# Another order of the seven score products in a planned decoder-layer kernel, and other durations for its planner

## The chip, the cores and the metric

The kernel runs on one core of a Trainium2 chip. Its engines are TensorE (PE, with its weight loads shown as PEld), VectorE (DVE), ScalarE (ACT), GpSimd (POOL) and the queue that issues the DMAs (SP). The metric is the device time of one execution in microseconds. The kernel before takes 2433.74 us, the median of three runs (2433.09 to 2435.8).

## The reference

One decoder layer over 2048 positions of width 1024, all in float32. A mixer (a gated linear recurrence and a convolution module side by side) is followed by cross-attention into 256 memory positions with four heads, and by a gated feed-forward of width 3072 with a short convolution; a norm ends it. The part that the change touches is the cross-attention:

```python
    h = rms_norm(x, xa_norm_g[l])
    m = rms_norm(mem, mem_norm_g[l])
    q = (h @ w_q[l]).reshape(bsz, s, XA_HEADS, XA_HD)
    kv = m @ w_kv[l]
    ...
    scores = jnp.einsum("bshd,bmhd->bhsm", q, k).astype(jnp.float32) * (XA_HD ** -0.5)
    p = jax.nn.softmax(scores, axis=-1).astype(v.dtype)
    o = jnp.einsum("bhsm,bmhd->bshd", p, v).reshape(bsz, s, d)
    x = x + o @ w_o[l]
```

## The kernel before, in words

**The stages.** The sequence is worked in two halves of 1024 positions. In `attend` (line 1373) each half passes through three large products, one after the other: the mixer's output times `w_out` (the order `FIRST`), the normed activations times a matrix A that holds `w_q` times the keys of all four heads (`SECOND`, the score products), and the probabilities times a matrix VO that holds the values times `w_o` (`THIRD`, the output products). While the first half's attention runs, the second half's recurrence and convolution run on VectorE and ScalarE beside it.

**Seven products for eight.** Each large product is 1024 by 1024 by 1024 and is cut into quarters of 512. `seven` (line 1228) makes it from seven products of 512 by 512 by 512, P1 to P7, whose operands are quarters or sums of quarters: S1 = A21 + A22, S2 = S1 - A11, S3 = A11 - A21, S4 = A12 - S2 on the left, T1 to T4 on the right. The results are gathered into the quarters C11, C12, C21 and C22. Each of the seven runs over four inner blocks `i` (groups) and four blocks of 128 positions `tb`. Every operand is split into a rounded high part and a low rest, so each pair of blocks takes three matmuls of 128 by 128 by 512: 12 matmuls in a group.

**Banks.** A product's four blocks of positions lie in four of the eight banks of PSUM. The orders name them "a" or "b", and say whether the product starts fresh (True) or adds to what the banks hold (False). P1, P6 and P7 add up in "a", and each state of the sum is taken out on the way; P5 and P3 add up in "b". The names after that are the quarters that the product's result goes to. The number `held` counts the banks in use; the recurrences put their gate matmuls only where it is at most 4 (line 990).

**Scores and probabilities.** `score` (line 1432) takes a product's banks: the first result of a quarter is copied to SBUF by ScalarE (tile `prob`), every later one is added by VectorE. With the last one, `softmax` (line 1263) follows for that block of 128 positions: VectorE finds the maximum of two heads, ScalarE takes two exponentials with sums, VectorE the reciprocals, ScalarE scales the two parts. A quarter has four such blocks. `turn` (line 1399) transposes a quarter of probabilities on TensorE, 16 transposes into four banks, and `take_p` (line 1443) copies these out on ScalarE (tile `pt`). The rounding of `pt` gives `yh` on ScalarE, and `yl` on VectorE: the left operands of the output products. The last argument of `seven` says after which product and group such work is put into the program, counted from 0: (6, 0) is after the first group of the seventh product.

**The planner.** The program is not run in the order in which it is written. Every instruction is recorded with its operands (`Program`), and `schedule` (line 320) simulates the five engines with estimated durations (`estimate`, line 66), a hop of 0.3 us between engines, DMA rates, table switches on ScalarE and the free slots of SBUF and PSUM. On each engine the ready instruction with the earliest due time goes first. Due times are worked back from when TensorE wanted the results in the pass before (`deadlines`, line 283). `emit` (line 466) makes 28 passes, takes the pass with the least estimated end, and emits each engine's instructions in that order. All instructions are emitted by one line, so the profile gives line 485 for all of them and is read by the names of tiles.

Of the kernel before, what the change touches and what calls it, by code (L numbers as in the profile page):

```python
# [62 lines left out]
STACKS = 2  # L63


def estimate(eng, name, n, pointer):
    if eng == "DVE":
        if name == "reciprocal":
            return 0.1 + n * 0.0063
        return (0.13 if name == "scalar_tensor_tensor" else 0.08) + n * 0.00104  # L70
    if eng == "Pool":
        return 0.18 + n * 0.0021
    return 0.1 + n * 0.00083 + 0.09 * pointer


class Buf:
# [90 lines left out]
class Program:  # L167
# [51 lines left out]
    def do(self, eng, name, out, *args, reads=(), writes=(), **kw):  # L219
        outs = [out] + ([kw["accum_out"]] if "accum_out" in kw else [])  # L220
        ins = [a for a in list(args) + list(kw.values()) if isinstance(a, Ref) and a not in outs]
        if eng == "PE":
            o = self.group or self.op("PE")
            n = ins[1].n if name == "matmul" else P
            if name == "matmul":
                cost = (n + 32) / 2400.0 if ins[1].rounded else n * 4 / 2400.0
            else:
                cost = 0.11
            self.clock += cost
            o.cost += cost  # L230
        else:
            o = self.op("Pool" if eng == "either" else eng)
            o.either = eng == "either"
            n = max(r.n for r in ins + outs)
            o.cost = estimate(o.eng, name, n, any(isinstance(a, Ref) for a in kw.values()))
            if eng == "DVE":
                self.vector = max(self.vector, self.clock) + o.cost
            if eng == "ACT":
                o.sets = ACT_SETS.get(args[1])
        o.calls.append((name, (out,) + args, kw))  # L240
        for r in outs:
            if not r.rounded:
                r.buf.loaded = False
        self.touch(
            o, [b for r in ins for b in r.parts()] + [b.parts[0] for b in reads],
            [b for r in outs for b in r.parts()] + [b.parts[0] for b in writes],
        )
# [72 lines left out]
    def schedule(self):  # L320
# [9 lines left out]
        def push(t, kind, x):  # L330
            seq[0] += 1
            heapq.heappush(events, (t, seq[0], kind, x))
# [35 lines left out]
        def pick(e, t):  # L368
            h = ready[e]
            while h and h[0][2].start is not None:  # L370
                heapq.heappop(h)
            if not h:
                return None
            if e == "Pool":
                back, o, wake = [], None, None
                while h and o is None:
                    x = heapq.heappop(h)
                    if x[2].start is not None:
                        continue
                    spare = x[2].due + lag[0] - POOL_LAST - t  # L380
                    if x[2].either and spare > 0:
                        back.append(x)
                        wake = spare if wake is None else min(wake, spare)
                    else:
                        o = x[2]
                for x in back:
                    heapq.heappush(h, x)
                if o is None and wake is not None:
                    push(t + max(wake, 0.2), 3, e)
                return o  # L390
            if e == "ACT":
                o = h[0][2]
                if o.sets is not None and table[0] not in o.sets and o.due + lag[0] - t > ACT_PATIENCE:
                    other = [x for x in h if x[2].sets is None or table[0] in x[2].sets]
                    if other:
                        x = min(other)
                        h.remove(x)
                        heapq.heapify(h)
                        return x[2]
            return heapq.heappop(h)[2]  # L400

        def dispatch(e, t):
            if not idle[e]:
                return
            o = pick(e, t)
            if o is None:
                return
            idle[e] = False
            o.start, o.on = t, e
            order.append(o)  # L410
            if e == "PE":
                lag[0] += 0.2 * (t - o.turn - lag[0])
            cost = o.cost
            if e == "ACT" and o.sets is not None and table[0] not in o.sets:
                cost += ACT_SWITCH
                table[0] = o.sets[0]
            if o.either and e == "DVE":
                cost = estimate("DVE", "tensor_tensor", 1024, False)
            if e == "SP":
                dma_free[0] = max(dma_free[0], t) + cost  # L420
                push(max(t + 0.1, dma_free[0] - BACKLOG), 2, e)
                push(dma_free[0] + o.delay, 0, o)
            else:
                push(t + cost, 2, e)
                push(t + cost, 0, o)
# [16 lines left out]
        while events:  # L442
            t, _, kind, o = heapq.heappop(events)
            end = max(end, t)
            if kind == 1:
                for e in (["DVE", "Pool"] if o.either else [o.eng]):
                    heapq.heappush(ready[e], (o.due, o.idx, o))
                    dispatch(e, t)
            elif kind == 3:
                dispatch(o, t)  # L450
            elif kind == 2:
                idle[o] = True
                dispatch(o, t)
            else:
                for s in o.succs:
                    satisfied(s, t + (HOP_SAME if s.eng == o.on else HOP))
                for b in o.bufs:
                    b.left -= 1
                    if b.left == 0:
                        free[b.tag].append(b.slot)  # L460
                        grant(b.tag, t + HOP)
# [51 lines left out]
def hybrid_layer(  # L513
# [31 lines left out]
    def transpose(o, in_, idn):  # L545
        pr.do("PE", "transpose", o, in_, idn)
# [8 lines left out]
    def ps():  # L555
        return pr.new("ps", name="ps")
# [630 lines left out]
    class Blocks:  # L1187
# [5 lines left out]
        def get(self, key, i):  # L1193
            if key[0] == "A":
                return self.raw[int(key[1]) - 1, int(key[2]) - 1, i]
            if (key, i) not in self.s:
# [4 lines left out]
    C11, C12, C21, C22 = (0, 0), (0, 1), (1, 0), (1, 1)  # L1201
    PRODUCTS = dict(P1=("A11", "B11"), P2=("A12", "B21"), P3=("S4", "B22"), P4=("A22", "T4"), P5=("S1", "T1"), P6=("S2", "T2"), P7=("S3", "T3"))
    FIRST = (("P1", "a", True, [C11]), ("P2", "b", True, [C11]), ("P6", "a", False, [C12]), ("P5", "b", True, [C22]),
             ("P7", "a", False, [C22]), ("P3", "b", False, [C12]), ("P4", "a", False, [C21]))
    SECOND = (("P1", "a", True, [C11]), ("P4", "b", True, [C21]), ("P2", "b", True, [C11]), ("P6", "a", False, [C12]), ("P5", "b", True, [C22]),
              ("P7", "a", False, [C21, C22]), ("P3", "b", False, [C12]))
    THIRD = (("P1", "a", True, [C11]), ("P4", "b", True, [C21]), ("P6", "a", False, [C12]), ("P5", "b", True, [C22]),
             ("P7", "a", False, [C21, C22]), ("P2", "a", True, [C11]), ("P3", "b", False, [C12]))

# [163 lines left out]
    def attend(h, ready):  # L1373
# [10 lines left out]
        def pass_on(q):  # L1384
            return {} if not h else {0: [lambda: ys.append(scaled(q))], 1: [lambda: list(turned(ys.pop(), take_on(q)))]}
# [13 lines left out]
        def turn(src, th, half, take):  # L1399
            for k in range(KH):  # L1400
                p = ps()
                with together():
                    for tb in range(NTB):
                        transpose(p[:, tb * P : (tb + 1) * P], src[th, tb, half][:, k * P : (k + 1) * P], ident[:])
                take(th, half, k, p)

        def take(th, half, k, p):
            t = X.raw[th, half, k] = tmp("xa")
            ACT(t[:], p[:], AF.Copy, scale=vec["v1024"][:, half * KH + k, G_XA : G_XA + 1])
# [20 lines left out]
        prob, PT = {}, Blocks()  # L1430
# [12 lines left out]
        def take_p(th, half, k, p):  # L1443
# [3 lines left out]
        yield fours[1]  # L1447
        yield from seven(SECOND, X, A_Q, score, {
            (0, 1): [lambda: turn(xs, 1, 0, take), rates],
            (1, 3): pass_on(1).get(0, ()),  # L1450
            (3, 0): pass_on(1).get(1, ()),
            (6, 0): [lambda: turn(prob, 0, 0, take_p)],
        })
        del X
        st2 = [Stats(), Stats()]
# [9 lines left out]
        def norm_next(*steps):  # L1465
            return [conf_in[3], lambda: [step_norm(q) for q in (2, 3) for _ in range(len(steps))]] if not h else []
# [1 line left out]
        yield fours[2]  # L1468
        yield from seven(THIRD, PT, VO_Q, add2, {
            (0, 1): [lambda: turn(prob, 1, 1, take_p)],  # L1470
            (0, 3): [lambda: turn(prob, 1, 0, take_p)],
            (0, 2): norm_next(0, 1, 2),
            (2, 0): norm_next(3),
            (2, 2): [lambda: turn(prob, 0, 1, take_p)],
# [406 lines left out]
    fours.append(spawn(quads(VO_Q, PV, mem_vo), calm=CALM))  # L1881
    mixing = spawn(mixers())
    attends[0] = spawn(attend(0, [mixing, normeds[0], normeds[1], lru_out[1], fours[0]]))
    attends[1] = spawn(attend(1, [lru_out[3], attended[0]]))
    first = spawn(first_x(), attends[1])
    tail = spawn(feed_forward())
# [33 lines left out]
```

## Time and profile before

| | us |
|---|---|
| median of three runs | 2433.74 |
| the profiled execution | 2434.4 |
| its span, first to last instruction | 2432.6 |
| PE busy | 2399.2 |
| DVE busy | 1923.1 |
| ACT busy | 1278.8 |

The span is that of one profiled execution; 1.8 us of its own time lie around it. PE's matmuls are pipelined, and each row's duration reaches into the next one's start, so the distance between starts is the cost of a matmul. Where a row ends in square brackets, its engine was idle for so many microseconds before it, and what is named there came last.

| stretch | what runs there |
|---|---|
| about 610 to 702 us | score products of the first half |
| about 888 to 959 us | score products of the second half |
| from about 959 us | output products of the second half |

### The profile page before, as it was taken

Reading aid. Unit: us, or ns where it says so; the run is one execution under the profiler, and the core shown is the slowest. Engines: PE = TensorE matmul, PEld = TensorE weight load, DVE = VectorE, ACT = ScalarE, POOL = GpSimd, SP = SyncE. Lnnn points to the kernel's source line nnn. Section 1 sums busy time; section 2 is a strip of 40 time slices with the busy share of each in tenths; the row PEclk is TensorE's granted clock in tenths of the full one; section 3 lists DMA queues with packets and bytes.
Section 4 is the critical chain, followed back from the end, with each engine's and each line's share of the span. In section 5 each row is a group of like instructions: output and inputs, shape, how many; then the busy total and the mean of one; then the engine's idle time right before and its main releaser. Section 6 shows DMA issues by size and latency. Waiting matters only on the chain.

```text
span 2432.6 us, 32495 instructions
## 1 busy us (share of the span) xinstructions
PE 2399.2 (99%) x10788; PEld 1979.2 (81%) x10788; DVE 1923.1 (79%) x3231; ACT 1278.8 (53%) x2246; POOL 0.7 (0%) x6
## 2 busy tenths in 40 slices
PE   7999999999999999999999999999999999999998
PEld 6888778888777888788888888888888888888887
DVE  5699979999999545897988878988787585667656
ACT  7438567467796457585554446555444331233222
POOL 0000000000000000000000000000000000000000
PEclk9999999999999999999999999999999999999999
DMA  8988898989787957556655446654442397789774
GB/s 285 322 312 278 268 312 278 299 267 313 263 283 259 327 188 260 173 183 229 234 199 190 165 161 215 234 183 156 160 143 70 104 314 259 249 277 355 230 240 169
DMA packets 344063, 572.08 MB, mean 235 GB/s; under 512 B 33052, under 2 KB 110876, under 8 KB 343894
## 3 DMA queue, kind: packets, MB, share of 16 engines
q1 hardware_dynamic: 343894, 570.00, 69.4%
q8 instruction: 85, 1.39, 0.2%
q14 instruction: 84, 0.69, 0.1%
HBM read 385.32 MB, written 184.55 MB: 234 GB/s over the span
## 4 chain that ended last, share of the span: by engine, by line
PE 71%; ACT 3%; DVE 1%; issue 0%; DMA 0%; DVEq 0%; ACTq 0%
PE ps L485 71%; ACT prob L485 2%; ACT yh L485 0%; ACT L485 0%; ACT pt L485 0%; DVE yl L485 0%; DVE acc L485 0%; DMA VO<-VO 0%; DVE smalls L485 0%; DMA VO<-yh 0%; DVE conv L485 0%; DVE gate L485 0%; DVE prob L485 0%; ACT m L485 0%; ACT sq L485 0%
## 5 line engine op out<-in xcount | busy, mean ns | idle before, releaser
L485 PE MATMUL ps<-Xh,wh 128*128 128x512 f32 x1344 | 523.6, 390 | 0.0
L485 PE MATMUL ps<-Xh,wl 128*128 128x512 f32 x1344 | 522.9, 389 | 0.0
L485 PEld LDWEIGHTS ps<-Xh,wl 128*128 128x128 f32 x1344 | 252.3, 188 | 52.5
L485 PEld LDWEIGHTS ps<-Xh,wh 128*128 128x128 f32 x1344 | 252.3, 188 | 52.2
L485 PE MATMUL ps<-wh,yh 128*128 128x512 f32 x672 | 266.7, 397 | 7.8 <-ACT prob L485 4.5
L485 PE MATMUL ps<-wl,yh 128*128 128x512 f32 x672 | 263.5, 392 | 0.1
L485 PE MATMUL ps<-wh,yl 128*128 128x512 f32 x672 | 263.5, 392 | 0.0
L485 PE MATMUL ps<-wl,hidh 128*128 128x512 f32 x672 | 261.4, 389 | 0.0
L485 PE MATMUL ps<-wh,hidh 128*128 128x512 f32 x672 | 261.4, 389 | 0.0
L485 DVE TENSOR_TENSOR acc<-acc,ps 128x512 f32<-128x512 f32 x192 | 129.4, 686 | 148.6 <-PE ps L485 147.8
L485 PE MATMUL ps<-wh,hidl 128*128 128x512 f32 x624 | 242.7, 389 | 0.0
L485 PE MATMUL ps<-Xl,wh 128*128 128x512 f32 x576 | 224.1, 389 | 0.0
L485 PE MATMUL ps<-xh,wh 128*128 128x512 f32 x512 | 203.9, 398 | 0.0
L485 PE MATMUL ps<-xh,wl 128*128 128x512 f32 x512 | 199.6, 390 | 0.3 <-DVE wl L485 0.3
L485 PE MATMUL ps<-xl,wh 128*128 128x512 f32 x512 | 199.5, 390 | 0.0
L485 ACT ACTIVATE wh<-s 128x512 fp32r<-128x512 f32 x192 | 119.5, 627 | 117.1 <-DVE s L485 57.3
L485 ACT ACTIVATE u<-ps 128x512 f32<-128x512 f32 x144 | 85.7, 595 | 150.1 <-PE ps L485 136.0
L485 PEld LDWEIGHTS ps<-wh,yh 128*128 128x128 f32 x672 | 127.5, 190 | 34.4 <-ACT prob L485 5.0
L485 DVE TENSOR_TENSOR wl<-s,wh 128x512 fp32r<-128x512 f32 x192 | 130.5, 688 | 28.2 <-PE ps L485 14.8
L485 PE MATMUL ps<-xn,wh 128*128 128x512 f32 x384 | 149.4, 389 | 0.0
L485 PE MATMUL ps<-tx,wh 128*128 128x512 f32 x384 | 149.4, 389 | 0.0
L485 PEld LDWEIGHTS ps<-wh,yl 128*128 128x128 f32 x672 | 127.2, 189 | 26.9 <-DVE yl L485 0.2
(209 smaller groups left out, 4513.1 us busy)
## 6 DMA issues: line engine op xcount, KB each, us to landing
raw<-in_w_up_dram SPq DMA_DIRECT2D x96, 512.0 KB
wh<-w_down SPq DMA_DIRECT2D x164, 256.0 KB
wl<-w_down SPq DMA_DIRECT2D x164, 256.0 KB
hid<-cv SPq DMA_DIRECT2D x48, 512.0 KB
h<-hid SPq DMA_DIRECT2D x96, 256.0 KB
w_down<-wh SPq DMA_DIRECT2D x84, 256.0 KB
x<-in_x_dram SPq DMA_DIRECT2D x64, 256.0 KB
wh<-w_out SPq DMA_DIRECT2D x56, 256.0 KB
```

The lines of the kernel that those rows point to most:

```text
L485: getattr(e, name)(*[resolve(a) for a in args], **{k: resolve(a) for k, a in kw.items()})
```

## The change

It has three parts. In `SECOND`, P7 now comes ahead of P5: C21 and C22 take P7's result (C21's last, C22's first), and then P5's is C22's last. The turn of C21's probabilities moves from the output products, after the fourth group of the first one, to the score products, after the third group of the last one. And `estimate` gives other durations: for a reciprocal and a scan on VectorE, and on ScalarE 0.09 us for each operand that is a tile reference (scale, bias, accumulated sum) where it was 0.09 us if there was any. With these the whole order of the program is made afresh.

```diff
-def estimate(eng, name, n, pointer):
+def estimate(eng, name, n, pointers):
     if eng == "DVE":
         if name == "reciprocal":
-            return 0.1 + n * 0.0063
+            return 0.07 + n * 0.0063
+        if name == "tensor_tensor_scan":
+            return 0.13 + n * 0.00208
         return (0.13 if name == "scalar_tensor_tensor" else 0.08) + n * 0.00104
     if eng == "Pool":
         return 0.18 + n * 0.0021
-    return 0.1 + n * 0.00083 + 0.09 * pointer
+    return 0.1 + n * 0.00083 + 0.09 * pointers
...
-            o.cost = estimate(o.eng, name, n, any(isinstance(a, Ref) for a in kw.values()))
+            o.cost = estimate(o.eng, name, n, sum(isinstance(a, Ref) for a in kw.values()))
...
-    SECOND = (("P1", "a", True, [C11]), ("P4", "b", True, [C21]), ("P2", "b", True, [C11]), ("P6", "a", False, [C12]), ("P5", "b", True, [C22]),
-              ("P7", "a", False, [C21, C22]), ("P3", "b", False, [C12]))
+    SECOND = (("P1", "a", True, [C11]), ("P4", "b", True, [C21]), ("P2", "b", True, [C11]), ("P6", "a", False, [C12]), ("P7", "a", False, [C21, C22]),
+              ("P5", "b", True, [C22]), ("P3", "b", False, [C12]))
...
             (6, 0): [lambda: turn(prob, 0, 0, take_p)],
+            (6, 2): [lambda: turn(prob, 1, 0, take_p)],
...
             (0, 1): [lambda: turn(prob, 1, 1, take_p)],
-            (0, 3): [lambda: turn(prob, 1, 0, take_p)],
             (0, 2): norm_next(0, 1, 2),
```

More of the change, by code (lines that the diff above doesn't have):

```diff
@@ L417, in dispatch @@
             if o.either and e == "DVE":
-                cost = estimate("DVE", "tensor_tensor", 1024, False)
+                cost = estimate("DVE", "tensor_tensor", 1024, 0)
             if e == "SP":
```

## The prediction

> **What bounds the kernel now.** I read the page first: how busy each engine is over the span.
>
> ```profile
> span 2432.6 us, 32495 instructions
> ...
> PE 2399.2 (99%) x10788; PEld 1979.2 (81%) x10788; DVE 1923.1 (79%) x3231; ACT 1278.8 (53%) x2246; POOL 0.7 (0%) x6
> ```
>
> TensorE does nothing for 2432.6 - 2399.2 = 33.4 us. The change adds and removes no matmul, so all that it can win lies in those 33.4 us and in matmuls that run slowly. Next I read the busy time of the engines in stretches that I chose around the stages (columns: stretch, its length, then PE, PEld, DVE, ACT and POOL busy with instruction counts, the granted clock, DMA).
>
> ```profile
> 0.00:40.00 40.00, 27.66 (x146) 23.34 (x147) 21.71 (x78) 27.42 (x55) 0.70 (x6) 1.00 0.84 269
> 560.00:640.00 80.00, 75.25 (x352) 62.00 (x351) 80.00 (x129) 62.45 (x111) 0.00 (x0) 0.99 0.83 283
> 640.00:690.00 50.00, 48.75 (x219) 39.75 (x217) 49.48 (x99) 35.63 (x71) 0.00 (x0) 0.99 0.92 315
> 690.00:738.00 48.00, 43.99 (x198) 34.41 (x196) 44.77 (x93) 47.08 (x115) 0.00 (x0) 0.93 0.63 226
> 925.00:985.00 60.00, 57.11 (x264) 47.45 (x263) 34.63 (x80) 46.32 (x124) 0.00 (x0) 0.94 0.62 209
> 985.00:2390.00 1405.00, 1405.00 (x6241) 1164.20 (x6240) 1089.23 (x1729) 621.43 (x1024) 0.00 (x0) 1.00 0.62 208
> ```
>
> From 985 to 2390 us TensorE is never idle: a new order can only lose there. The start holds 12.3 us of idle time. The rest sits in three stretches, all in the attention of the two halves of the sequence: 560 to 738 us (first half) and 925 to 985 us (second half). In the first half VectorE is full (80.00 of 80, 49.48 of 50, 44.77 of 48) and ScalarE nearly so at the end (47.08 of 48). In the second half both have room: 34.63 and 46.32 of 60. The waits of TensorE say who came last:
>
> ```profile
> PE ps L485 <- ACT prob L485: 4.5, 1, 4.5
> PE ps L485 <- ACT pt L485: 3.4, 2, 2.9
> PE ps L485 <- ACT r L485: 2.8, 2, 2.1
> ```
>
> All three are ScalarE: copies of scores out of PSUM (prob), copies of turned probabilities (pt), and a norm's square root (r).
>
> **The stall in the second half, which the change aims at.** TensorE in order of time (start, duration, what, how many):
>
> ```profile
> 949.29 1.91 PE L485 MATMUL ps<-ident,prob 128*128 128x128 f32 x16
> 950.95 0.48 PE L485 MATMUL ps<-wh,yh 128*128 128x512 f32 x1
> ...
> 971.88 1.91 PE L485 MATMUL ps<-ident,prob 128*128 128x128 f32 x16
> 976.67 0.80 PE L485 MATMUL ps<-wh,yh 128*128 128x512 f32 x1 [2.89 <-ACT pt L485]
> 977.27 0.63 PE L485 MATMUL ps<-wl,yh 128*128 128x512 f32 x1
> ...
> 982.82 0.40 PE L485 MATMUL ps<-wh,yl 128*128 128x512 f32 x1
> ```
>
> Sixteen turns need 950.95 - 949.29 = 1.66 us. The turn at 971.88 is the quarter C21; it stands directly ahead of the second output product. That product needs four banks of PSUM, the first product holds four, and the turn has taken the other four, so it waits for ScalarE to empty them. At 976.67 it starts, and its first 14 matmuls, up to 982.82, are slow: 6.15 / 14 = 0.44 us apart. The full pitch is that of the stretch without a gap, 1405 us / 6241 = 0.225 us. The stall costs 982.82 - 971.88 - 1.66 - 14 x 0.225 = **6.1 us**. Why ScalarE is late:
>
> ```profile
> 923.04 0.58 ACT L485 ACTIVATE prob<-ps 128x512 f32<-128x512 f32 x1
> ...
> 924.11 1.06 ACT L485 ACTIVATE prob<-ps 128x512 f32<-128x512 f32 x2
> ...
> 925.64 0.59 ACT L485 ACTIVATE prob<-ps 128x512 f32<-128x512 f32 x1
> ...
> 949.92 1.09 ACT L485 ACTIVATE pt<-ps 128x512 f32<-128x512 f32 x2 [13.44 <-PE ps L485]
> ...
> 952.89 0.62 ACT L485 ACTIVATE prob<-prob,smalls 128x256 f32<-128x256 f32 x1
> ...
> 960.77 1.15 ACT L485 ACTIVATE yh<-pt 128x512 fp32r<-128x512 f32 x2
> ...
> 976.01 2.05 ACT L485 ACTIVATE pt<-ps 128x512 f32<-128x512 f32 x4
> ```
>
> ```profile
> 944.73 4.87 DVE L485 TENSOR_TENSOR prob<-prob,ps 128x512 f32<-128x512 f32 x8 [9.92 <-PE ps L485]
> ```
>
> ScalarE was idle for 13.44 us until 949.92, because the scores of C21 and of C22 both end with the sixth product, P7: its eight adds (944.73) start together, and then two softmax blocks queue one behind the other. One block of four tiles takes 960.77 - 952.89 = 7.9 us.
>
> **The change part by part.** A score product is 4 x 4 x 3 = 48 matmuls, 48 x 0.225 = 10.8 us. The instructions are the same ones: C22 now starts with P7 (four copies on ScalarE) and ends with P5 (four adds and the softmax), where it began with P5 and ended with P7; C21 ends with P7 as before. So nothing is removed or added on any engine, nor a DMA: the loads of the T1 and T3 weights on SP's queue swap places.
>
> *P7 ahead of P5.* C21's scores are done 10.8 us earlier. In the second half its 7.9 us block then fits into the 13.44 us in which ScalarE waited, and C22's block no longer stands behind it. *The turn of C21 two groups into the last score product.* It stands ahead of the first output product now, with two of that product's four groups (2 x 12 x 0.225 = 5.4 us) still to come to cover its four copies (2.05 us at 976.01), and the turn of C22 has the same 5.4 us behind it as before. The banks "a" are given up after P7, so four banks are in use while P5 runs, where eight were: room for turns. Load on ScalarE from P5's end to the second output product: C22's block 7.9, three turns' copies 3 x 2.05, and two sets of four roundings, which the 960.77 row prices at about 0.55 us each, 4.4: 18.5 us, under two products and two turns, 2 x 10.8 + 2 x 1.66 = 24.9 us. C12's block may follow. So the whole 6.1 us goes: **-6.1** (bounds -6.1 and 0).
>
> *What the swap adds: two hand-overs without a product between.* P6 and P7 use the same four banks, and so do P5 and P3; before, another product stood between each pair. Now P7's first matmul on a bank waits for the ScalarE copy that reads P6's sum from it, and P3's for VectorE's add. Queued behind a waiting matmul is all of TensorE, and behind it everything else. The second half can be priced from rows. Turn 949.29 stands one group (2.70 us) into P3, so P3 began at 946.6, P7 at 935.8 and P5, P6's follower, at 925.0. P6's copies ended at about 923.6, 924.6, 925.2 and 926.2; a follower on the same banks would want them at 925.0, 925.7, 926.3 and 927.0. All four are in time by 0.7 us or more, though softmax stood between them. The add at 944.73 takes 0.61 us of its group of eight and the bank is wanted at 946.6: in time by over 1 us. So the price is near 0; I take +0.3, bounds 0 and +1.2 (four banks by 0.3).
>
> *The first half.* Its stalls, and the copies that matter there:
>
> ```profile
> 633.71 0.39 PE L485 MATMUL ps<-wh,yl 128*128 128x512 f32 x1
> 638.63 0.80 PE L485 MATMUL ps<-wh,yh 128*128 128x512 f32 x1 [4.54 <-ACT prob L485]
> ...
> 641.66 0.40 PE L485 MATMUL ps<-wl,yh 128*128 128x512 f32 x1
> ...
> 688.43 0.63 PE L485 MATMUL ps<-ident,prob 128*128 128x128 f32 x4 [0.62 <-DVE prob L485]
> ...
> 723.93 1.98 PE L485 MATMUL ps<-sum,ones 128*128 128x512 f32 x4 [0.25 <-DVE x L485]
> 725.76 1.04 PE L485 MATMUL ps<-ident,prob 128*128 128x128 f32 x8
> ...
> 732.46 2.82 PE L485 MATMUL ps<-ident,prob 128*128 128x128 f32 x12 [0.56 <-ACT pt L485]
> 735.63 0.80 PE L485 MATMUL ps<-wh,yh 128*128 128x512 f32 x1 [0.35 <-ACT yh L485]
> ...
> 737.07 0.40 PE L485 MATMUL ps<-wh,yh 128*128 128x512 f32 x1
> ```
>
> ```profile
> 636.17 1.28 ACT L485 ACT_TABLE_LOAD   x1
> ...
> 638.00 0.58 ACT L485 ACTIVATE prob<-ps 128x512 f32<-128x512 f32 x1
> ...
> 663.85 0.58 ACT L485 ACTIVATE prob<-ps 128x512 f32<-128x512 f32 x1
> ...
> 665.89 1.28 ACT L485 ACT_TABLE_LOAD   x1
> ...
> 667.72 0.58 ACT L485 ACTIVATE prob<-ps 128x512 f32<-128x512 f32 x1
> ...
> 669.58 1.06 ACT L485 ACTIVATE prob<-ps 128x512 f32<-128x512 f32 x2
> ```
>
> The boundary between score and output products: from 723.93 to 737.07 there are four rows of ones (1.83 us, to 725.76), two turns (32 transposes, 3.3 us) and three matmuls (0.7 us). The stall is 13.14 - 5.8 = **7.3 us**. The third output product wants C21 turned, and its turn sits there beside a norm's banks. With C21's scores 10.8 us earlier and its turn placed earlier, this should ease. But the cover is thin: ScalarE has 50 - 35.63 = 14.4 us free between 640 and 690, enough for one block of 7.9, while VectorE, which must add and reduce first, has 0.5 us. Gone entirely or not at all, the bounds are -7.3 and 0; between them I take about half, **-4**.
>
> At 633.71 the third score product waits for banks that ScalarE empties only from 638.00 on, behind a table load. It costs 641.66 - 633.71 less eight matmuls (1.8), **6.1 us**. The swap does not touch it; only the order made afresh can. I take -2, bounds -6.1 and +6.1 (a second one like it). The hand-over of P6 to P7 here: the four copies run from 663.85 to 670.64, with a table load between, where banks come free within 3 x 0.68 us. They could wait then because P5 followed on other banks. Now they are due at once and are ordered by due time, so I take +1.5 for both hand-overs, bounds 0 and +6.1 for each (the 633.71 row is the same kind of wait).
>
> *Durations.* The order is written by a list scheduler that runs the program on its own durations, 28 passes, and keeps the pass with the least estimated end. The new ones lengthen each Exp of a softmax by two pointers, 0.18 us, so 8 x 0.18 = 1.4 us a block, and the scan from 0.61 to 1.20 us. The 7.9 us block is 8 x (0.58 + 0.40) = 7.9 by the new numbers and 6.4 by the old. The planner thus sees ScalarE as full as it is; this is what lets me count half of the first-half stall. Every engine's order over the program is remade, at the start too (12.3 us idle); I take 0, bounds -2 and +3: nothing more can be won between 985 and 2390.
>
> Sum, against the profiled execution's own time of 2434.4 us (the span and 1.8 around it): -6.1 + 0.3 - 4 - 2 + 1.5 = -10.3, **2424.1**. The median of the three runs is 2433.7, 0.7 lower; from it 2423.4. I say 2424.
>
> One rule against this: the Trainium skill, "TensorE: Matmul & The Clock Gate", section "A second HAM failure mode: psum-queue depth-cycling", says that small idle gaps between groups of matmuls, from cycling through PSUM banks, can make the clock swing between half and full. By it the new hand-overs would cost far more than their waits. The trace does not bear it out for short gaps: after the 0.62 us at 688.43 four transposes took 0.63 us, while at the half clock of 732.46 twelve took 2.82.
>
> **The rivals.** Second half only: the first half stays as it is, or gains in one place and loses in another. For it speaks the full VectorE from 560 to 690 us. Then -6.1 + 0.3 and up to 3 us of new waits: 2428 to 2431; most of this is within 0.2% of the time before, 4.9 us, which is about what a measurement of this kernel can tell from no change. That the edit does not do what it says belongs here: TensorE's order is the planner's, and a turn may stay where it was; 2434.
>
> All stalls of the attention go: 2433.7 - 6.1 - 6.1 - 7.3 - 1.1 (the small waits near 688) = 2413. For it: the planner now knows the blocks. Against: VectorE at 80.00 of 80.
>
> On the other side, slower: late hand-overs in the first half. Place: P6 to P7 and P5 to P3 between about 660 and 700 us, where ScalarE loads tables between copies and VectorE is full. Price: the 633.71 stall for each, 6.1, so -6.1 + 12.2 = +6.1: 2440. It decides from 5.5 us a hand-over (6.1 + 4.9, halved), and needs ScalarE to run a table load and several other instructions ahead of copies that are due, as it did ahead of 638.00.
>
> The swinging clock: each of four hand-overs followed by 14 matmuls at half clock, as after 976.67: 4 x 14 x 0.2 = 11.2, so -10.3 + 11.2 = +0.9: 2435. The rule named above would bring this; the row at 688.43 speaks against it.
>
> **How the numbers follow.** My forecast 0.55 (0.52 of it under 2428.9), all stalls gone 0.13, second half only 0.17 (same), slower hand-overs 0.10, the clock 0.05 (0.03 same, 0.02 slower). Faster 0.52 + 0.13 = 0.65; same 0.03 + 0.17 + 0.03 = 0.23; slower 0.12. The forecast's own range is 2418 to 2430. The range for 8 in 10 takes in nearly all of the case without stalls and the second-half case, and leaves out the slower hand-overs: 2414 to 2437.
>
> **What would show it.** Second half: no wait of TensorE for pt before the second output product, and a clock of 1.00 where it was 0.94; one softmax block on ScalarE while P5 runs; the adds in two groups of four 10.8 us apart. First half: the boundary wait shorter; P6's copies within some 3 us of each other; no half-clock matmuls at P7's or P3's start. The prediction is wrong if TensorE waits for prob at those starts by more than 1 us in the second half, if a new stall over 3 us appears outside 560 to 985 us, or if the first-half waits add up to more than before.

## The result and the profile after

The changed kernel takes 2419.32 us (median of five runs, 2417.07 to 2421.74), 0.9941 of the time before (95% interval 0.9930 to 0.9952): 14.4 us faster. 2424 was forecast, with 2414 to 2437 as the range. The profiled execution took 2419.32 us, its span 15.1 us less than before.

```profile
span 2417.5 us, 32315 instructions
...
PE 2392.8 (99%) x10788; PEld 1978.0 (82%) x10788; DVE 1923.6 (80%) x3231; ACT 1277.3 (53%) x2246; POOL 0.7 (0%) x6
```

The counts of matmuls and of VectorE's and ScalarE's instructions are the same. The stretches of the prediction, for the kernel after:

```profile
560.00:640.00 80.00, 76.73 (x356) 62.98 (x355) 79.51 (x130) 60.88 (x107) 0.00 (x0) 0.98 0.84 281
640.00:690.00 50.00, 49.00 (x222) 40.26 (x221) 49.97 (x104) 45.62 (x94) 0.00 (x0) 0.99 0.95 328
690.00:738.00 48.00, 48.00 (x230) 38.74 (x229) 47.20 (x94) 47.91 (x108) 0.00 (x0) 1.00 0.73 243
...
925.00:985.00 60.00, 60.00 (x297) 50.57 (x296) 44.94 (x92) 45.90 (x114) 0.00 (x0) 1.00 0.63 206
```

TensorE is now full from 690 to 738 us and from 925 to 985 us, at the full clock (1.00, where it was 0.93 and 0.94). What is left lies from 560 to 690 us, 3.3 + 1.0 us idle, at the start, and in 7.5 us behind the last matmul, which the kernel before has too. No wait for probabilities is among TensorE's waits any more:

```profile
PE ps L487 <- ACT mem L487: 7.5, 2, 6.7
PE ps L487 <- DMA raw<-in_ffn_norm_g_dram: 3.2, 1, 3.2
PE ps L487 <- DMA raw<-in_w_q_dram: 2.2, 1, 2.2
PE ps L487 <- DVE hlast L487: 1.8, 1, 1.8
PE ps L487 <- ACT xh L487: 1.2, 1, 1.2
PE ps L487 <- DVE yl L487: 1.2, 2, 1.0
```

The first three are at the start of the program; the last three in the first half. In the second half ScalarE's queue, in order of time, shows the new place of C21's softmax:

```profile
924.87 2.64 ACT L487 ACTIVATE prob<-ps 128x512 f32<-128x512 f32 x4 [0.76 <-PE ps L487]
930.18 0.60 ACT L487 ACTIVATE prob<-prob,smalls 128x256 f32<-128x256 f32 x1 [2.68 <-DVE smalls L487]
...
934.87 3.30 ACT L487 ACTIVATE prob<-prob,smalls 128x256 f32<-128x256 f32 x8
940.95 2.07 ACT L487 ACTIVATE pt<-ps 128x512 f32<-128x512 f32 x4 [2.78 <-PE ps L487]
```

The copies at 924.87 are C22's, at P7's end. One block runs from 930.18 to about 938.1, while P5 runs, which is now the product ahead of P3; in the kernel before, ScalarE was idle during the product ahead of P3 (the 13.44 us up to 949.92). The longest idle time in front of any of these rows is 2.78 us. On VectorE the adds come in two groups, C21's at P7's end and C22's at P5's, where eight started together before:

```profile
925.50 2.73 DVE L487 TENSOR_TENSOR prob<-prob,ps 128x512 f32<-128x512 f32 x4 [0.51 <-ACT prob L487]
...
935.75 1.37 DVE L487 TENSOR_TENSOR prob<-prob,ps 128x512 f32<-128x512 f32 x2 [0.58 <-PE ps L487]
...
937.63 1.27 DVE L487 TENSOR_TENSOR prob<-prob,ps 128x512 f32<-128x512 f32 x2
```

The turns that follow on TensorE (C11, C21 and C22) have no wait behind them:

```profile
940.31 1.91 PE L487 MATMUL ps<-ident,prob 128*128 128x128 f32 x16
947.52 1.91 PE L487 MATMUL ps<-ident,prob 128*128 128x128 f32 x16
957.46 1.91 PE L487 MATMUL ps<-ident,prob 128*128 128x128 f32 x16
```

In the first half the turn of C21 has left the boundary. Its 16 transposes begin at 693.95, inside P3, and at the boundary, where the kernel before had two turns one behind the other, one is left, that of C12:

```profile
693.95 1.49 PE L487 MATMUL ps<-ident,prob 128*128 128x128 f32 x12
...
733.81 1.47 PE L487 MATMUL ps<-ident,prob 128*128 128x128 f32 x12
```

### The profile page after: what moved, and what is told of

Its sections match the earlier page's. It is cut to its first block, busy times and chain, and to the rows that moved or that the text cites. A ratio compares the mean times of both kernels' runs of the same rounds, so it can differ in the third digit from the quotient of the medians.

```text
span 2417.5 us, 32315 instructions
## 1 busy us (share of the span) xinstructions
PE 2392.8 (99%) x10788; PEld 1978.0 (82%) x10788; DVE 1923.6 (80%) x3231; ACT 1277.3 (53%) x2246; POOL 0.7 (0%) x6
## 4 chain that ended last, share of the span: by engine, by line
PE 72%; DVE 0%; DVEq 0%; issue 0%
PE ps L487 72%; DVE acc L487 0%; DVE yl L487 0%; DVEq L1917 0%; DVE smalls L487 0%
```

## The experiments

Three theories were set against each other. **By places:** the swap and the turn clear the stalls where the probabilities are due. **By durations:** a planner with true durations clears them whatever the order of the products. **By draw:** a planner that makes the whole order afresh loses another amount in the first half with every change, whatever the change means. For each kernel the table has the median time and the idle time of TensorE in four stretches, each its length less TensorE's busy time in the row of that stretch (0 to 60 us: the start; 540 to 680: the score products of the first half; 680 to 780: their boundary with the output products; 925 to 1025: the same boundary in the second half).

| kernel | swap | turn | durations | us | 0-60 | 540-680 | 680-780 | 925-1025 |
|---|---|---|---|---|---|---|---|---|
| before | no | no | old | 2433.7 | 12.4 | 5.5 | 5.1 | 2.9 |
| before, hop 0.31 | no | no | old | 2439.2 | 14.8 | 3.1 | 13.4 | 2.9 |
| durations only | no | no | new | 2427.7 | 12.4 | 4.8 | 5.3 | 0.7 |
| swap, no turn | yes | no | new | 2427.7 | 14.8 | 2.2 | 8.3 | 0.3 |
| turn, no swap | no | yes | new | 2436.1 | 11.3 | 7.0 | 6.4 | 3.0 |
| old durations | yes | yes | old | 2424.0 | 13.0 | 5.8 | 2.6 | 0 |
| scan only | yes | yes | scan | 2422.9 | 14.1 | 6.9 | 1.0 | 0 |
| pointers only | yes | yes | pointers | 2421.8 | 13.6 | 4.8 | 0.8 | 0 |
| after | yes | yes | new | 2419.3 | 12.9 | 4.3 | 0 | 0 |
| after, 27 passes | yes | yes | new | 2417.9 | 12.2 | 4.3 | 0 | 0 |
| after, hop 0.31 | yes | yes | new | 2427.7 | 12.2 | 9.3 | 2.1 | 0 |
| P2 between | yes | yes | new | 2424.4 | 14.6 | 7.4 | 0.4 | 0 |
| output swap | yes | yes | new | 2422.9 | 13.1 | 6.7 | 0.5 | 0 |

The idle time leaves out matmuls at half clock, so a row's sum is less than its loss.

**Old durations.** Swap and turn as after; `estimate` as before.

```diff
-        if name == "tensor_tensor_scan":
-            return 0.13 + n * 0.00208
...
-    return 0.1 + n * 0.00083 + 0.09 * pointers
+    return 0.1 + n * 0.00083 + 0.09 * bool(pointers)
```

> P7 ahead of P5 and the turn of C21 in the score products, but the planner's durations as before. Three theories. By places: the swap and the turn take the second half's 6.1 us away by themselves and the new durations took the first half's; then this kernel has no stall between 925 and 985 us, keeps some 15 us of losses between 560 and 740 us, and takes about 2428 us. By durations: true durations alone did it all; then the stall of the second half is still there and the time is 2431 to 2434. By draw: any order made afresh loses another amount in the first half, between 5 and 16 us; then the second half is clean and the time lies anywhere from 2418 to 2429.

2424.0 us, 0.9959 of before (0.9947 to 0.9972). The second half is clean without new durations, as by places, and the boundary of the first half halves; the first-half loss (5.8 + 2.6 us idle) is less than that theory gave, so the time lies below the 2428 of "by places" and within what "by draw" allowed. The risk that the prediction named shows here: ScalarE's queue at the end of P6 in the first half, and TensorE in front of P7.

```profile
659.91 1.28 ACT L485 ACT_TABLE_LOAD   x1
661.20 0.63 ACT L485 ACTIVATE m<-m 128x512 f32<-128x512 f32 x1
661.74 0.58 ACT L485 ACTIVATE prob<-ps 128x512 f32<-128x512 f32 x1
662.21 0.62 ACT L485 ACTIVATE yh<-s 128x512 fp32r<-128x512 f32 x1
662.73 0.59 ACT L485 ACTIVATE prob<-ps 128x512 f32<-128x512 f32 x1
```

```profile
660.20 0.39 PE L485 MATMUL ps<-wh,yl 128*128 128x512 f32 x1
662.37 0.50 PE L485 MATMUL ps<-wh,yh 128*128 128x512 f32 x1 [1.78 <-ACT prob L485]
```

The first of P6's four copies starts at 661.74, behind a table load and a square root, and the next matmul starts when it ends: a direct hand-over cost 1.78 us here.

**Durations only.** The products and the turn as before, `estimate` as after.

```diff
-    SECOND = (... ("P6", "a", False, [C12]), ("P7", "a", False, [C21, C22]),
-              ("P5", "b", True, [C22]), ("P3", "b", False, [C12]))
+    SECOND = (... ("P6", "a", False, [C12]), ("P5", "b", True, [C22]),
+              ("P7", "a", False, [C21, C22]), ("P3", "b", False, [C12]))
...
-            (6, 2): [lambda: turn(prob, 1, 0, take_p)],
...
+            (0, 3): [lambda: turn(prob, 1, 0, take_p)],
```

> The new durations with the old order of products (P5 ahead of P7) and the old place of the turn. By places: the first half is as after the change (about 7 us lost between 560 and 740 us), the stall ahead of the second output product in the second half is back with 6 us: 2425. By durations: no stall in the second half either, 2419 to 2421. By draw: the second half loses about 6 us and the first half anything from 5 to 16: 2423 to 2434.

2427.7 us, 0.9976 (0.9967 to 0.9985). The time is within what "by draw" allowed, but no theory had the places: the second half's stall is down to 0.7 us of idle time with the old order of products, nearly as "by durations" said, and the first half's boundary stays at 5.3, against it. So in the second half the old order of products does not have to stall, though it did in the kernel before.

**Swap without turn.** New durations and swap, the turn back in the output products.

```diff
-            (6, 2): [lambda: turn(prob, 1, 0, take_p)],
...
+            (0, 3): [lambda: turn(prob, 1, 0, take_p)],
```

> New durations and P7 ahead of P5, but C21 turned after the fourth group of the first output product, as before. If the early softmax is what matters: ScalarE has its work on C21 done when the turn comes, the four copies of the turn are all that the second output product waits for, 1 to 2.5 us in each half, and the time is 2421 to 2424. If the place of the turn is what matters (it fills the last four banks right ahead of that product): a stall of 3 us or more with half clock behind it, 5 to 6 us, 2425 or more. If neither: 2419.

2427.7 us, 0.9975 (0.9966 to 0.9984). The second half is clean to 0.3 us: there the early softmax is enough. The first half's boundary is not, as TensorE shows:

```profile
724.35 1.14 PE L487 MATMUL ps<-ident,prob 128*128 128x128 f32 x8 [0.62 <-ACT r L487]
732.18 1.11 PE L487 MATMUL ps<-ident,prob 128*128 128x128 f32 x4 [6.69 <-ACT prob L487]
734.26 2.82 PE L487 MATMUL ps<-ident,prob 128*128 128x128 f32 x12 [0.96 <-ACT pt L487]
```

With C21's turn back in its old place, two turns stand at the boundary one behind the other again (32 transposes, from 721.84 on), and the second waits 6.69 us for its probabilities. The turn's place counts for more there than was expected.

**Turn without swap.** New durations and the early turn, P5 ahead of P7 again.

```diff
-    SECOND = (... ("P6", "a", False, [C12]), ("P7", "a", False, [C21, C22]),
-              ("P5", "b", True, [C22]), ("P3", "b", False, [C12]))
+    SECOND = (... ("P6", "a", False, [C12]), ("P5", "b", True, [C22]),
+              ("P7", "a", False, [C21, C22]), ("P3", "b", False, [C12]))
```

> New durations and the turn of C21 in the last score product, but P5 ahead of P7 as before. C21's scores then come 10.8 us later, so that its block of softmax (7.9 us), C22's and the turns fall into the last score product. If the early turn is enough: 2419 to 2421. If the swap is needed: TensorE waits for the probabilities ahead of the first or second output product in the second half, 3 to 8 us: 2423 to 2428.

2436.1 us, 1.0011 (1.0003 to 1.0020): slower than expected and no better than before, with 3.0 us idle in the second half again. An early turn whose scores come late brought nothing in this order. That it does harm, 8.4 us above "durations only", is not shown, as a difference that means nothing moves a time by as much (under "The draw").

**Scan only, pointers only.** Swap and turn, and one of the new durations each: in the first `0.09 * bool(pointers)` and the old reciprocal, in the second no line for the scan and the old reciprocal.

> Swap and turn as after the change; of the new durations only the scan's. By durations: with softmax blocks still planned too short the first half loses some 12 us, as with all old durations: 2423 to 2425. By draw: the boundary between score and output products and the second half stay clean, the stretch from 580 to 670 us loses another amount between 4 and 11 us: 2417 to 2426.

> Swap and turn; of the new durations only ScalarE's pointers. By durations: this is the part that makes the planner see the softmax blocks at their true 7.9 us, so the result is that of the whole change within 2 us: 2418 to 2421. By draw: anything from 2417 to 2426, with no tie to which duration was kept.

2422.9 us, 0.9955 (0.9938 to 0.9971), and 2421.8 us, 0.9952 (0.9937 to 0.9966). The intervals lie on each other and on that of the whole change. The pointers are not shown to be the part that matters. Both orders have late hand-overs of P6 to P7 in the first half: TensorE waits 0.54 and 0.88 us with the scan only, and 1.92 us with the pointers only, where eight matmuls 0.43 us apart follow.

```profile
660.79 0.50 PE L485 MATMUL ps<-wh,yh 128*128 128x512 f32 x1 [1.92 <-ACT prob L485]
```

**The draw.** Two kernels that differ from the one after in one constant of the planner, and one that differs so from the kernel before:

```diff
-PASSES = 28
+PASSES = 27
```

```diff
-HOP = 0.3
+HOP = 0.31
```

> The changed kernel with 27 planning passes where it has 28: the products, places and durations are the same, at most the pass that is kept differs. By durations: within 2 us of 2419, or the very same order. By draw, if another pass is kept: up to 6 us away, from the stretch 580 to 670 us alone.

> The changed kernel with the planner's hop between engines at 0.31 us where it was 0.30: a disturbance that is as good as the old value. By durations: 2417 to 2421. By draw: 2417 to 2426, boundary and second half still clean (under 2 us lost there), the stretch from 580 to 670 us anywhere from 4 to 11 us.

> The kernel before with the planner's hop at 0.31 us: its old products, places and durations under another draw. If the swap and the turn are what cleared the boundary of the first half and the second half: both still stall here, 4 us or more of idle time between 680 and 780 us and 1 to 3 between 925 and 1025 us, 2428 to 2440. If those stalls were one unlucky order: under 2 us in each, 2424 or less.

With 27 passes the order of every engine is the same as after, so 2417.9 us (0.9938, 0.9923 to 0.9953) is a second sample of one program: they agree to 1.4 us. With the hop at 0.31 us the changed kernel takes 2427.7 us (0.9976, 0.9967 to 0.9985), 8.4 us more than after. That is above the range of both theories, by 1.7 us for "by draw". Its extra idle time is where "by draw" put it, from 540 to 680 us, with 2.1 us at the boundary:

```profile
540.00:680.00 140.00, 130.66 (x586) 105.93 (x586) 138.92 (x233) 107.11 (x183) 0.00 (x0) 0.98 0.85 282
680.00:780.00 100.00, 97.92 (x456) 79.63 (x455) 99.18 (x185) 85.16 (x198) 0.00 (x0) 1.00 0.77 261
```

The kernel before with the same hop takes 2439.2 us (1.0022, 1.0013 to 1.0032), 5.5 us more than before, and stalls at both boundaries, 13.4 and 2.9 us, as was expected if the swap and the turn cleared them. So with this hop too the whole change is faster, by 11.5 us where it was 14.4:

```profile
680.00:780.00 100.00, 86.58 (x392) 69.02 (x391) 95.88 (x177) 84.21 (x187) 0.00 (x0) 0.95 0.71 239
925.00:1025.00 100.00, 97.11 (x462) 81.11 (x461) 65.10 (x128) 66.85 (x163) 0.00 (x0) 1.00 0.63 210
```

**P2 between.** P2 is put between P6 and P7, so that P6's copies have a product of time (the turned norm moves with P6).

```diff
-... ("P2", "b", True, [C11]), ("P6", "a", False, [C12]), ("P7", "a", False, [C21, C22]),
+... ("P6", "a", False, [C12]), ("P2", "b", True, [C11]), ("P7", "a", False, [C21, C22]),
...
-            (3, 0): pass_on(1).get(1, ()),
+            (2, 0): pass_on(1).get(1, ()),
```

> New durations and the early turn, but the order P1, P4, P6, P2, P7, P5, P3: P2 stands between P6 and P7, so the copies of P6 have a whole product of time again, and C21 still ends before P5. (The turned norm of the first half's output moves with P6 by one product.) If the direct hand-over from P6 to P7 costs nothing, as the changed kernel's trace says: 2417 to 2423, by the draw of the first half alone. If it holds back ScalarE's other work in the first half (the 580 to 670 us stretch): 3 to 6 us less there, 2413 to 2416.

2424.4 us, 0.9958 (0.9941 to 0.9975): 1.4 us above the range of its first expectation and no gain. To take away the hand-over that the prediction feared bought nothing that can be told from a draw (7.4 us idle from 540 to 680 us).

**Output swap.** P7 ahead of P5 in `THIRD` as well.

```diff
-    THIRD = (... ("P6", "a", False, [C12]), ("P5", "b", True, [C22]),
-             ("P7", "a", False, [C21, C22]), ("P2", "a", True, [C11]), ("P3", "b", False, [C12]))
+    THIRD = (... ("P6", "a", False, [C12]), ("P7", "a", False, [C21, C22]), ("P5", "b", True, [C22]),
+             ("P2", "a", True, [C11]), ("P3", "b", False, [C12]))
```

> The changed kernel with P7 ahead of P5 in the output products too, which makes two more direct hand-overs there, P6 to P7 and nothing between P7 and P5, with VectorE's adds as the reader. If a hand-over costs nothing where the reader has room: the second half's output products stay without a wait, and the time is 2417 to 2424 by the first half's draw. If hand-overs cost 0.3 us or more a bank: 2 to 5 us of waits for x between 960 and 1040 us, 2421 or more.

2422.9 us, 0.9959 (0.9944 to 0.9974). No idle time from 925 to 1025 us: with VectorE reading the banks, and busy for 77.7 of these 100 us, the direct hand-over is free there too.

**Less on VectorE.** The second half's convolution over 16 of 31 taps.

```diff
-        for i in range(NE):
+        for i in range(NE if h == 0 else NE // 2):
```

> The changed kernel, but the convolution of the second half of the sequence runs over 16 of its 31 taps only (the rest of the computation is as before, the output is not the layer's). It runs on VectorE beside the first half's attention: 4 channel blocks x 8 steps x 3 instructions x 0.66 us = 63 us less there. If the 4 to 9 us of idle time that every order has between 540 and 680 us come from a full VectorE: under 1.5 us of idle time there, 2411 to 2415. If they come from the planner's order or from ScalarE's table loads: 4 us or more stay, 2417 or more.

2418.6 us, 0.9943 (0.9926 to 0.9959): no faster than after, where 2411 to 2415 was expected. The stretch, cut at 580 us:

```profile
540.00:580.00 40.00, 37.49 (x173) 30.65 (x172) 38.36 (x66) 30.11 (x52) 0.00 (x0) 1.00 0.93 302
580.00:680.00 100.00, 100.00 (x467) 83.48 (x466) 78.29 (x141) 87.79 (x158) 0.00 (x0) 1.00 0.92 314
```

```profile
PE ps L487 <- DMA wh<-w_out: 2.3, 1, 2.3
```

From 580 to 680 us, with VectorE at 78 of 100 us, TensorE is never idle; every kernel of the table has at least 2.2 us of idle time from 540 to 680. But one wait of 2.3 us for a load of `w_out` weights has come in ahead of it, and the start has 13.9 us of idle time where it had 12.9. So it speaks for the full VectorE as the cause of the waits after 580 us, in one order only, and it does not show that the time would follow.

## Why the prediction was right, and where its terms were off

*The second half, -6.1.* Right: no idle time and full clock from 925 to 985 us, one softmax block during P5, the adds in two groups. All seven orders of the table with swap and turn have 0 there. What the working missed is that the swap is not the only way: under new durations the old order had only 0.7 us idle. And 3 of the 6.1 us were matmuls at half clock, which the kernel before with hop 0.31 did not have behind an equal wait (last section). Two counts in the working were off and did no harm. The early turn stands after the third group of P3, so one group (2.7 us) and not two is left to cover its copies of 2.05 us: in the trace they end at 950.2, and P3 at about 952. And three turns, not two, lie between P5's end and the second output product, 1.66 us more room than was counted.

*Hand-overs in the second half, +0.3.* 0. The price that the prediction read from the old copies' times, near 0, was right.

*The boundary in the first half, -4.* This term was mis-sized: all of its 7.3 us went, and with it the small waits near 688, 1.1 us. The prediction took half because VectorE had only 0.5 us free there. The rows after show that a full VectorE did not stand in the way: from 640 to 690 it works 49.97 of 50 us. ScalarE now works 45.62 us of these 50, where it worked 35.63, but that is not what clears the boundary: with the pointers only it works 33.72 us there, and the boundary has 0.8 us idle.

```profile
640.00:690.00 50.00, 48.09 (x214) 39.59 (x213) 49.13 (x101) 33.72 (x66) 0.00 (x0) 0.97 0.82 275
```

Seven different orders with swap and turn have 0 to 2.6 us idle there, five without the pair 5.1 to 13.4; the pair is shown to be the cause there, and the one order of each part alone has 8.3 and 6.4 us.

*The stall at 633.71, -2.* About -1: that stall is gone, but others of 1.25 and 1.82 us stand near it, and the stretch from 540 to 680 us went from 5.5 to 4.3 us of idle time. Across all orders of the table it has 2.2 to 9.3 us, with or without any part of the change.

*Hand-overs in the first half, +1.5.* 0 in the changed kernel; in the same products 1.8 us under old durations, 1.9 with the pointers only and 1.4 with the scan only. The term was of the right size for three orders and absent in others. It is not absent because the copies were prompt. Of P6's four, the last two start at 664.16, over 4 us after the first, where some 3 us was to be the sign:

```profile
659.97 0.57 ACT L487 ACTIVATE prob<-ps 128x512 f32<-128x512 f32 x1
...
664.16 1.06 ACT L487 ACTIVATE prob<-ps 128x512 f32<-128x512 f32 x2
```

```profile
662.44 0.51 PE L487 MATMUL ps<-wh,yl 128*128 128x512 f32 x1 [1.00 <-DVE yl L487]
```

P7 begins at 660.81, and its only wait is one of 1.00 us for a rounding on VectorE; none is for a copy. Its first twelve matmuls, up to 664.64, start before the third copy can have ended (0.57 us after 664.16), so they all lie in the two banks that were already copied: the planner put matmuls of P7's second group on these ahead of the first group's on the late two.

*Durations and the order made afresh, 0 with -2 and +3.* At the start +0.5 us. For the whole, the bounds were too narrow: one hundredth of a microsecond in the hop moved 8.4 us. That the time came within 5 us of the forecast is thus in part luck, as the order with hop 0.31 takes 2427.7 us, on the other side of 2424. That the new durations brought the rest of the gain (the 4.7 us between old durations and after) is not shown. After with hop 0.31, the same durations, is 3.7 us slower than old durations.

The sum by places: -6.1 - 7.3 - 1.1 - 1.2 + 0.5 = -15.2, and the span fell by 15.1. The last two terms are idle time alone, without slow matmuls, so the sum agrees better than its terms are known. Of the rivals, "all stalls of the attention go" came nearest in kind; its 2413 assumed that the 633.71 stall goes too. The swinging clock did not come in the changed kernel. Late hand-overs came in three other orders, at up to a third of the price in waiting, once with matmuls at half clock behind (pointers only).

## What to carry to other kernels

Where two blocks of work for one engine become ready at the same moment behind an engine that must not wait, look for a product that can be moved so that one of them becomes ready earlier, and move its consumer with it: here, under the new durations, the first alone gave no time (2427.7 us with and without it) and the second alone none either. A direct hand-over of a buffer cost from 0 to 1.9 us of waiting here, by what stood ahead of the copy in its reader's queue; check that queue, not the number of hand-overs. And when a planner writes the order, measure a few orders that differ by nothing that matters before a difference of some microseconds is given to a parameter.

## What was not expected of the hardware

**Equal waits, different clocks.** In the kernel before, the 2.89 us wait in front of 976.67 was followed by 14 matmuls 0.44 us apart. The kernel before with hop 0.31 has the same wait behind the same turn:

```profile
978.51 1.91 PE L485 MATMUL ps<-ident,prob 128*128 128x128 f32 x16
983.31 0.50 PE L485 MATMUL ps<-wh,yh 128*128 128x512 f32 x1 [2.89 <-ACT pt L485]
983.64 0.40 PE L485 MATMUL ps<-wl,yh 128*128 128x512 f32 x1
983.88 0.40 PE L485 MATMUL ps<-wh,yl 128*128 128x512 f32 x1
```

Here the matmuls follow at 0.33 and 0.24 us: the wait cost some 3 us and not 6.1. In the kernel after, shorter waits brought the half clock:

```profile
633.85 0.50 PE L487 MATMUL ps<-xh,gwah 128*128 128x512 f32 x1 [1.25 <-ACT xh L487]
636.17 0.50 PE L487 MATMUL ps<-xl,gwah 128*128 128x512 f32 x1 [1.82 <-DVE hlast L487]
...
637.81 0.63 PE L487 MATMUL ps<-wl,yh 128*128 128x512 f32 x1
638.24 0.63 PE L487 MATMUL ps<-wh,yl 128*128 128x512 f32 x1
```

Eight matmuls from 637.81 on are 0.43 us apart. Behind hand-overs it was the same: eight matmuls 0.43 us apart followed the wait of 1.92 us with the pointers only, and none the 1.78 us under old durations. The prediction's reading, that short gaps leave the clock alone, held for its 0.62 us row and not for these. The Trainium skill, "TensorE: Matmul & The Clock Gate", Part 1, says that the window in which activity is judged runs freely, and that the point of a change depends on where in it the first matmul lands. The equal waits with unequal clocks would fit this; no run here shows the window itself. The same part gives, for the change to half clock, at least one idle window of about 3.4 us. The waits here do not fit that figure: 2.89 us alone, and 1.25 and 1.82 us with a matmul between.

**The start moves by itself.** The same program waited 2.2 us for `in_w_q_dram` in one profiled execution (after), and 1.0 us in the other (27 passes).

```profile
PE ps L487 <- DMA raw<-in_w_q_dram: 1.0, 1, 1.0
```
